# Eight state buffers for heads 1 to 3, stores ahead of the sums, and a distance in the planner for TensorE's work at the ends of six chains

## The chip, the core and the metric

One Trainium2 chip, one of its cores. The metric is the device time of one execution in microseconds (us). TensorE multiplies matrices, VectorE (DVE in the rows) and ScalarE (ACT) do the elementwise work, GpSimd (POOL) does little here, and SyncE (SP) issues nearly all transfers, in one queue, in order.

## The reference

One decoding step of one layer for 512 prompt tokens and 8 sample tokens, which share all weights:

```
z   = rmsnorm(h) @ w_in                     # 1024 -> q,k,v of 12 heads; q,k,v,gates of 4 mLSTM heads
o_a = dilated sliding-window attention      # prompt: 128-wide blocks; samples: rows of three caches
q,k = silu(causal_conv(z_q, z_k))           # mLSTM, 4 heads of 256
samples, each head and sample:
    C_new = w_x * C + w_i * outer(k, v)     # C is 256 x 256, read and written
    num   = q . C_new
prompt: the same recurrence over 512 tokens, as masked products
h  += (sig(ga) * (o_a @ w_pa) + sig(gb) * (o_b @ w_pb)) @ w_out
h  += (silu(x @ w_gate) * (x @ w_up)) @ w_down
h  += sig(x @ w_pg) * (p @ w_pp);  y = rmsnorm(h)
```

All caches and states are outputs too, moved on by one token.

## The kernel before

Activations lie as 128 features by 520 tokens (512 + 8). A weight block of 128 x 128 is split into a high and a low part (`whi`, `wlo`) and meets the two parts of the activations in three matmuls of 260 columns for each half of the tokens; these "dense" matmuls fill most of the time. The list `order` fixes their order: w_in first (attention columns, then the mLSTM heads 0 to 3, then gates), then w_pa, w_pb, w_out, w_gate and w_up, w_down, w_pp, w_pg. The matmuls of w_pb and of most of w_gate and w_up go by Strassen-Winograd products (`wino`), whose raw weights land in buffers of the tags `rp`, `cA`, `cB` (and `WK` later).

All other work is generators ("processes") that the builder steps while it emits the dense matmuls. The class `Clock` estimates, as the program is built, when every engine is done with what was emitted; `on(engines, tiles, tag=n)` gives a condition: n buffers of the tag are free, and the tiles are ready by that estimate. A process goes on when its condition holds; what it emits then stands in the engines' queues at that place, for good. For TensorE (`engs[0] == "pe"`) the condition is that the tiles are ready at the estimated time at which TensorE takes its next matmul:

```
            if engs[0] == "pe":
                t = now
            ...
            return all(ck.ready(x) <= t for x in tiles)
```

If the estimate is early, TensorE comes to the matmul before its operand is there, and waits on the chip; nothing behind it in its queue can pass. If no dense matmul can go on, the builder moves the estimate in steps of 0.1 us (`stall`).

Six ends of chains matter here. `ev_conv` (L950): after the convolution, the tanh and a product with a row of weights (`kw`, in the buffer `yc`, with its sum in `nout`), four transposes of `kw` on TensorE; eight times. `attn_prompt` (L1126): a matmul with `E` and one with `t`, twice each, between small VectorE operations. `attn_sample` (L1201): transposes of the normalised scores `sc`, once (in the trace `scs`). `sample_rows` (L1335): transposes of the sample rows `qkm`, four times. `sample_sums` (L1408): a matmul with `nt`, four times.

The sample states run as a stream beside all this. `sample_loads(h)` (L1353) loads, for each pair of samples, rows of q and k spread over all partitions into the buffers `P1` and `P2` (two each), and for each sample the state `ct` (256 KB) into a buffer of the tag `S` (five). `mlstm_sample(h)` (L1370) scales the state, adds two outer products in place, and then takes two sums over it with q (`tensor_tensor_reduce`, into `numv`); after the sums a process for the store is begun, and the buffer is given back when the store is emitted. The tag `S` also serves the cache rows of `attn_sample` (`kvb`, `qb`) and the rows of `sample_rows`. The loads of heads 1 to 3 begin once `attn_sample` has asked for its last cache rows. After the sums of head 3, `sample_sums` sets `("ns", 3)`, without which no raw weight goes into `cA`; `sample_out` and `pieces` then make the last operand of the first w_pb product.

The tag `rp` (two buffers of 128 x 520) holds the tables `rC` and `rS` of the rotary embedding, read by `ev_rope` (L885) for the last of twelve blocks in the attention columns of half 1; `sw` is a scratch buffer of `ev_rope`. Both tags are free from then until w_pb (`rp`) and the feed-forward layer (`sw`).

Of the kernel before, what the change touches and what calls it, by code (L numbers as in the profile page):

```python
# [8 lines left out]
F32 = mybir.dt.float32  # L9
# [220 lines left out]
def _body(nc, a, const, sb, psp, drp):  # L230
    ck = Clock()
# [4 lines left out]
              P1=2, P2=2, cm=2, on=2, W0=2, W1=2, W2=2, W3=2, hm=2, sm=4, sm48=4,  # L236
              pp=2, b1=4, hf=3)
    WIDTH = dict(cA=640, cB=512, W1=384, W2=256, W3=128, raw=512, hi=512, lo=512, zc=ZC, yc=ZC - 3)
    used = dict.fromkeys(("pp", "G", "WK", "b1", "z", "y", "zc", "yc", "S", "P1", "P2", "cm", "hm", "hf", "sw"), 0)

    def tl(tag, name, shape=None, dt=F32):
        w = WIDTH.get(tag, 520)
        if tag in used:
            used[tag] += 1
        return ck.new(sb.tile(list(shape or (128, w)), dt, name=name, tag=tag, bufs=NB[tag]), tag, NB[tag])

# [17 lines left out]
    def free(n, tag):  # L264
        used[tag] -= n
# [2 lines left out]

    P = dict(PAR["A"])

    def on(engs, *tiles, lim=None, **rooms):

        engs = engs.split()

        def ok():
            for tag, n in rooms.items():
                if tag in used and used[tag] + n > NB[tag]:
                    return False
            now = ck.t["pe"]
            for tag, n in rooms.items():  # L280
                i = ck.count.get(tag, 0)
                if any(ck.idle(tag, i + j, NB[tag]) > now + P["SLACK"] for j in range(n)):
                    return False
            if engs[0] == "pe":
                t = now
            else:
                t = min(ck.t[e] for e in engs)
                if t > now + (P["LIM"] if lim is None else lim):
                    return False
                t = max(t, now) + 0.1  # L290
            return all(ck.ready(x) <= t for x in tiles)
        return ok
# [271 lines left out]
    def dma_chunk():  # L564
        c = dma_at[0]
        j, ci = order[c]
        dma_at[0] += 1
        if "src" in j:
            for b in j["load"].get(ci, ()):
                tag = next(j["tags"])  # L570
                wlast[tag, ck.count.get(tag, 0) % NB[tag]] = c - ci + WLAST[b]
                j["raw"][b] = tl(tag, "raw", (128, 4, 128))[:, :j["nk"]]
                SP.dma_start(j["raw"][b], j["src"][b])
            return
        src, _, n = j["chunks"][ci]
        if j["keep"] and (j["keep"], ci) in kept:
            return
        if j["keep"]:
            kept[j["keep"], ci] = None
        raw = tl("raw", "raw", (128, 4, 128))  # L580
        SP.dma_start(raw[:, :n, :j["M"]], src)
        raws[c] = raw
# [182 lines left out]
    eps_t = const.tile([128, 1], F32, name="eps_t")  # L765
    ident = cstA[:, C_ID:C_ID + 128]
    rC, rS = tl("rp", "rC"), tl("rp", "rS")
    rb = const.tile([128, 520], F32, name="rb")
    flag = {}
    HS = [slice(h * TH, h * TH + TH) for h in range(2)]  # L770
# [114 lines left out]
    def ev_rope(kind, g, i):  # L885
        def gen(ps):
            yield on("dve", rC, rS, ps, lim=P["EVLIM"], z=1, sw=1)
            z = tl("z", "z")
            sw = tl("sw", "sw")
            V.stream_shuffle(p2(sw), ps, SW)  # L890
            V.tensor_tensor(p2(z), ps, p2(rC), op=ALU.mult)
            free(1, "pp")
            yield on("dve", sw)
            mul(sw, sw, rS)
            yield on("dve", sw, z)
            add(z, z, sw)
            free(1, "sw")
            if g == 0:
                yield on("act dve", z, G=2)
                hi, lo = (tl("G", "qk"[kind] + x, (128, TP), F32R) for x in "hl")  # L900
                split(hi, lo, z[:, :TP])
                attn[kind, g, i] = hi, lo
            else:
                yield on("act dve", z, G=1)
                t = tl("G", "qk"[kind] + "r", (128, TP))
                copy(t.rearrange("p (r j) -> p r j", r=4), z[:, :TP].rearrange("p (j r) -> p r j", r=4))
                attn[kind, g, i] = t,
            G_.tensor_copy((qs, ks)[kind][:, i, g], z[:, TP:])
            if kind == 1:
                yield on("sp", z)  # L910
                SP.dma_start(a["kT"][2 * g + i], z)
            free(1, "z")
        return gen
# [36 lines left out]
    def ev_conv(h, w, dt):  # L950
        m = 8 * w + 2 * h + dt

        def gen(ps):
# [28 lines left out]
            if w == 0:  # L982
                free(1, "yc")
            else:
                kw = y[:, :TP]
                yield lambda: h in wkbs
                yield on("dve", y, wkbs[h])
                V.tensor_tensor_reduce(kw, kw, wkbs[h], sc, 0.0, ALU.mult, ALU.add, nout[:, h, dt, 0:1])
                if dt == 1:
                    free(1, "y")  # L990
                yield on("pe", kw, b1=1, WK=2)
                hi = tl("WK", "kwh", (128, 4, 128), F32R)
                lo = tl("WK", "kwl", (128, 4, 128), F32R)
                bk = bank((128, 4, 128))
                for s in range(4):
                    PE.transpose(bk[:, s], kw[:, s * 128:(s + 1) * 128], ident)
                free(1, "yc")
                yield on("act dve", bk)
                split(hi, lo, bk)
                free(1, "b1")  # L1000
                ml["kw", h, dt] = hi, lo
# [119 lines left out]
    done = {}  # L1121
# [4 lines left out]
    def attn_prompt(i):  # L1126
# [12 lines left out]
        yield on("dve", *st, y=1)  # L1139
        E = tl("y", "E", (128, 512))  # L1140
        V.tensor_copy(E.rearrange("p (j r) -> p j r", r=4), ident.unsqueeze(2).to_broadcast([128, 128, 4]))
        yield on("pe", E, b1=1)
        al = bank((128, 4, 2, 2, 4))
        for qb in range(4):
            PE.matmul(al[:, qb].rearrange("p c h r -> p (c h r)"),
# [24 lines left out]
        for lay in range(2):  # L1170
# [2 lines left out]
        t = one(32, "t32").rearrange("p (q h r) -> p q h r", q=4, h=2)  # L1173
        V.tensor_tensor(t, ex[:, 1].unsqueeze(3).to_broadcast([128, 4, 2, 4]),
                        cstB[:, C_R4:C_R4 + 4].unsqueeze(1).unsqueeze(1).to_broadcast([128, 4, 2, 4]), op=ALU.mult)
        yield on("pe", t, b1=1)
        w1 = bank((128, 2, 4))
        for qb in range(4):
            PE.matmul(w1.rearrange("p h r -> p (h r)"), cstB[:, C_Z + 96 - 32 * qb:C_Z + 224 - 32 * qb],
# [21 lines left out]
    def attn_sample():  # L1201
# [59 lines left out]
        for g in range(3):  # L1261
            yield on("pe", le)
            for i in range(2):
# [18 lines left out]
        rsv = rs[0:32].rearrange("p (g b) -> p g b", g=3)  # L1282
        V.tensor_tensor(rsv, cstB[0:32, C_M8:C_M8 + 8].unsqueeze(1).to_broadcast([32, 3, 8]),
                        sc[:, :, 128:129].to_broadcast([32, 3, 8]), op=ALU.mult)
        yield on("pe", sc, b1=1)
        bk = bank((128, 3, 32))
        for g in range(3):
            PE.transpose(bk[:, g], sc[:, g, 0:128], ident[0:32, 0:32])
# [42 lines left out]
    junk = const.tile([128, 256], mybir.dt.bfloat16, name="junk")  # L1331

    mdr, cts, qks = {}, {}, {}

    def sample_rows(h):  # L1335

        yield lambda: all(("k", h, dt) in ml for dt in range(2)) and "rows" in flag
        yield on("pe", qkm, b1=1, S=1)
        bk = bank((8, 2, 2, 128))
        rows = tl("S", "mrows", (8, 2, 256))  # L1340
        for w in range(2):
            for dt in range(2):
                PE.transpose(bk[:, w, dt], qkm[:, h, w, dt], ident)
        yield on("act dve", bk)
        copy(rows.rearrange("b w d -> b (w d)"), bk.rearrange("b w t d -> b (w t d)"))
        free(1, "b1")
        yield on("sp", rows)
        dr = drp.tile([8, 2, 256], F32, name="mdr", tag="mdr", bufs=2)
        SP.dma_start(dr.rearrange("b w d -> b (w d)"), rows.rearrange("b w d -> b (w d)"))
        free(1, "S")  # L1350
        mdr[h] = dr

    def sample_loads(h):  # L1353

        yield lambda: h in mdr
        dr = mdr[h]
        for b in range(8):
            if b % 2 == 0:
                yield on("sp", dr, P1=1, P2=1)
                qb, kb = tl("P1", "qb", (128, 2, 256)), tl("P2", "kb", (128, 2, 256))  # L1360
                SP.dma_start(qb, dr[b:b + 2, 0].partition_broadcast(128))
                SP.dma_start(kb, dr[b:b + 2, 1].partition_broadcast(128))
                qks[h, b] = qb, kb
            yield on("sp", S=1)
            ct = tl("S", "ct", (128, 2, 256))
            SP.dma_start(ct, a["sC"][h, b])
            cts[h, b] = ct
        flag["loads", h] = True

    def mlstm_sample(h):  # L1370
# [7 lines left out]
        def steps(b0):  # L1378
            for b in range(b0, 8, 2):
# [8 lines left out]
                for vt in range(2):  # L1388
                    yield on("dve", cur, kb, vw)
                    stt(cur[:, vt], kb[:, b % 2], vw[:, vt, b:b + 1], cur[:, vt], ALU.mult, ALU.add)  # L1390
                for vt in range(2):
                    yield on("dve", cur, qb)
                    V.tensor_tensor_reduce(junk, cur[:, vt], qb[:, b % 2], 1.0, 0.0, ALU.mult, ALU.add,
                                           numv[:, vt, b:b + 1])
                left[0] -= 1
                done[b] = True
                if b ^ 1 in done:
                    free(1, "P1")
                    free(1, "P2")
                store(a["C_s"][h, b], cur, lambda: free(1, "S"))  # L1400

        done = {}
        for b0 in range(2):
# [4 lines left out]
    def sample_sums(h, numv):  # L1408
# [8 lines left out]
        V.tensor_tensor(nn, nn, tv, op=ALU.add)  # L1417
        V.tensor_tensor(tv, nn, qkm[:, h, 0], op=ALU.mult)
        V.tensor_tensor(nt[:, :, 8:16], numv, numv, op=ALU.mult)
        yield on("pe", nt, b1=1)  # L1420
        bk = bank((128, 16))
        for t in range(2):
            PE.matmul(bk, ones, nt[:, t], start=t == 0, stop=t == 1)
# [388 lines left out]
    def pair_src(name, q):  # L1812
        return {f"{r + 1}{k + 1}": a[name][2 * q + r, k] for r in range(2) for k in range(2)}

    wok["cA"] = lambda: "scores" in flag and "oas" in flag and ("ns", 3) in ml and 1 in oaf
    wok["WK"] = lambda: order_pos[0] >= n_pa

# [463 lines left out]
```

## Time and profile before

| | |
|---|---|
| time, median of 3 runs | 1072.8 us (1072.44 to 1077.44) |
| profiled execution: its time, its span | 1072.9 us, 1071.1 us |
| TensorE matmul busy, share of the span | 1041.0 us, 97% |
| VectorE busy, ScalarE busy | 848.3 us (79%), 518.3 us (48%) |
| mean granted TensorE clock | 0.99 |
| HBM read, written | 163.65 MB, 59.13 MB |

The span is from the first to the last instruction; the time of the execution is 1.8 us longer. Busy time is the sum over an engine's instructions; matmuls overlap and their ends are modelled, so a busy TensorE need not run at its peak. The granted clock is 1.00 at 2.4 GHz and 0.50 at 1.2 GHz.

### The profile page before, as it was taken

The numbers are of one execution on the slowest core, as the hardware profiler recorded it, in microseconds if no ns is written. First come the engines' busy times: TensorE is split into PE (matmuls) and PEld (weight loads), VectorE is DVE, ScalarE is ACT, GpSimd is POOL, SyncE is SP. The second block draws the span as 40 slices with busy tenths as digits, with TensorE's granted clock in tenths as the row PEclk, the third lists the DMA queues.
The fourth block names the chain that finished last, engine by engine and source line by source line (L and its number), as shares of the span: only waits on it lengthen the run. The fifth ranks groups of instructions, "written<-read, shape, count | busy, mean of one in ns | idle before, by whom it ended". The sixth has DMA issues, their size and how long they took to land.

```text
span 1071.1 us, 21842 instructions
## 1 busy us (share of the span) xinstructions
PE 1041.0 (97%) x8440; PEld 1022.7 (95%) x8440; DVE 848.3 (79%) x1749; ACT 518.3 (48%) x963; POOL 40.8 (4%) x126
## 2 busy tenths in 40 slices
PE   8999999999998999999999999999999999999996
PEld 7999999898997999999999999999999999999995
DVE  6994678877797698998457588989788888866685
ACT  6534644555454477776333345444334334433652
POOL 0010010001010021000000000000000000000000
PEclk9999999999997999999999999999999999999999
DMA  6456247774865876987666743422332332333331
GB/s 227 129 181 211 85 147 261 258 223 155 265 192 179 294 268 230 296 273 259 219 204 230 257 125 87 145 79 75 114 113 76 114 111 75 108 91 105 99 110 60
DMA packets 91191, 180.21 MB, mean 168 GB/s; under 512 B 11636, under 2 KB 37796, under 8 KB 89680
## 3 DMA queue, kind: packets, MB, share of 16 engines
q1 hardware_dynamic: 90512, 178.29, 51.6%
q8 instruction: 66, 1.08, 0.4%
q10 hardware_dynamic: 576, 0.53, 0.1%
q14 instruction: 37, 0.30, 0.1%
HBM read 163.65 MB, written 59.13 MB: 208 GB/s over the span
## 4 chain that ended last, share of the span: by engine, by line
PE 77%; DVE 12%; DMA 5%; ACT 3%; issue 2%; SPq 0%; POOL 0%; DVEq 0%; ACTq 0%
PE pp L225 45%; PE b L225 32%; DMA raw<-in_w_in 2%; DVE wlo L225 2%; DMA ct<-in_sC 2%; DVE yc L225 2%; DVE ct L225 1%; DVE sw L225 1%; DVE Wf L225 1%; ACT whi L225 1%; DVE z L225 1%; DVE junk L225 1%; SPq L225 0%; DMA kvb<-in_cache 0%; DMA xr<-in_xT 0%
## 5 line engine op out<-in xcount | busy, mean ns | idle before, releaser
L225 ACT CAST whi<-raw 128x512 fp32r<-128x512 f32 (+3 forms) x344 | 204.9, 599 | 279.9 <-PE pp L225 146.3
L225 DVE TENSOR_TENSOR wlo<-raw,whi 128x512 fp32r<-128x512 f32 (+3 forms) x359 | 236.3, 661 | 129.4 <-ACT whi L225 121.2
L225 PE MATMUL b<-piece,whi 128*128 128x260 f32 x1176 | 212.3, 282 | 1.5 <-DVE whi L225 1.4
L225 PE MATMUL pp<-xnh,whi 128*128 128x260 f32 x992 | 204.2, 287 | 0.0
L225 PE MATMUL pp<-xnh,wlo 128*128 128x260 f32 x992 | 203.5, 287 | 0.0
L225 PE MATMUL pp<-xnl,whi 128*128 128x260 f32 x992 | 199.7, 283 | 0.0
L225 PEld LDWEIGHTS b<-piece,whi 128*128 128x128 f32 x1176 | 181.3, 188 | 1.9 <-issue 1.9
L225 PE MATMUL b<-piece,wlo 128*128 128x260 f32 x588 | 166.3, 283 | 0.1
L225 PEld LDWEIGHTS pp<-xnh,wlo 128*128 128x128 f32 x992 | 153.7, 190 | 1.0
L225 PEld LDWEIGHTS pp<-xnh,whi 128*128 128x128 f32 x992 | 153.0, 189 | 1.3
L225 PEld LDWEIGHTS pp<-xnl,whi 128*128 128x128 f32 x992 | 153.5, 189 | 0.0
L225 PEld LDWEIGHTS b<-piece,wlo 128*128 128x128 f32 x588 | 110.7, 188 | 0.4 <-DVE wlo L225 0.4
L225 PE MATMUL pp<-hpl,whi 128*128 128x260 f32 x352 | 71.1, 283 | 0.0
L225 PE MATMUL pp<-hph,whi 128*128 128x260 f32 x352 | 70.9, 283 | 0.0
L225 PE MATMUL pp<-hph,wlo 128*128 128x260 f32 x352 | 70.7, 282 | 0.0
L225 PEld LDWEIGHTS pp<-hph,wlo 128*128 128x128 f32 x352 | 54.4, 188 | 0.0
L225 PEld LDWEIGHTS pp<-hpl,whi 128*128 128x128 f32 x352 | 54.3, 188 | 0.0
L225 PEld LDWEIGHTS pp<-hph,whi 128*128 128x128 f32 x352 | 54.2, 188 | 0.0
L225 ACT CAST whi<-ws 128x512 fp32r<-128x512 f32 x28 | 17.4, 622 | 57.0 <-PE b L225 48.8
L225 DVE TENSOR_TENSOR uv<-uv,b 128x260 f32<-128x260 f32 (+1 forms) x84 | 40.8, 486 | 0.0
L225 DVE SCALAR_TENSOR_TENSOR yc<-zc,par,yc 128x552 f32<-128x552 f32 x48 | 37.8, 788 | 3.4 <-ACT yc L225 2.9
L225 PE MATMUL b<-x3h,wlo 128*128 128x260 f32 x128 | 36.7, 287 | 0.0
(387 smaller groups left out, 1933.3 us busy)
## 6 DMA issues: line engine op xcount, KB each, us to landing
raw<-in_w_in SPq DMA_DIRECT2D x132, 256.0 KB, 2.8
out_kvout<-in_cache SPq DMA_DIRECT2D x64, 512.0 KB, 4.8
raw<-in_w_gate SPq DMA_DIRECT2D x44, 256.0 KB, 2.9
raw<-in_w_up SPq DMA_DIRECT2D x44, 256.0 KB, 4.2
ct<-in_sC SPq DMA_DIRECT2D x32, 256.0 KB, 6.7
out_C_s<-ct SPq DMA_DIRECT2D x32, 256.0 KB, 4.9
raw<-in_w_down SPq DMA_DIRECT2D x32, 256.0 KB, 2.7
out_kvout<-in_cache SPq DMA_DIRECT2D x16, 510.0 KB, 3.9
```

The source lines that it names most:

```text
L225: fn(*args, **kw)
```

## The change

1. `on` gets `lead`: for TensorE the tiles must be ready, by the planner's estimate, at `now - lead`. It is 1.0 us at the transposes of `kw`, 0.8 us at the other five ends.
2. Of the eight states of each of the heads 1 to 3, the first two go to `rp`, the third to `sw`, five to `S`. Head 0 keeps `S`. `rp` is now counted: given back after the twelfth rotary block, taken for states, and raw weights of w_pb go to it only when the loads of head 3 are all emitted and no state holds it (`wok["rp"]`). Raw weights are not counted (`count=False`).
3. The process that stores a state is begun after the two outer products, ahead of the two sums. The buffer is given back when both the store and the sums are emitted (`both`, `release`).

```
-    def on(engs, *tiles, lim=None, **rooms):
+    def on(engs, *tiles, lim=None, lead=0.0, **rooms):
...
-                t = now
+                t = now - lead
...
+            ropes.append(z)
+            if len(ropes) == 12:
+                free(2, "rp")
...
-                yield on("pe", kw, b1=1, WK=2)
+                yield on("pe", kw, lead=1.0, b1=1, WK=2)
...
-        yield on("pe", E, b1=1)
+        yield on("pe", E, lead=0.8, b1=1)
...
-        yield on("pe", t, b1=1)
+        yield on("pe", t, lead=0.8, b1=1)
...
-        yield on("pe", sc, b1=1)
+        yield on("pe", sc, lead=0.8, b1=1)
...
+    release = {}
+
+    def both(cur, n):
+
+        left, tag = [n], ck.slot[cur.tensor.name][0]
+
+        def done():
+            left[0] -= 1
+            if not left[0]:
+                free(1, tag)
+        release[cur.tensor.name] = done
+        return done
...
-        yield on("pe", qkm, b1=1, S=1)
+        yield on("pe", qkm, lead=0.8, b1=1, S=1)
...
-            yield on("sp", S=1)
-            ct = tl("S", "ct", (128, 2, 256))
+            tag = ("rp", "rp", "sw", "S", "S", "S", "S", "S")[b] if h else "S"
+            yield on("sp", **{tag: 1})
+            ct = tl(tag, "ct", (128, 2, 256))
...
+                store(a["C_s"][h, b], cur, both(cur, 2))
...
-                store(a["C_s"][h, b], cur, lambda: free(1, "S"))
+                release[cur.tensor.name]()
...
-        yield on("pe", nt, b1=1)
+        yield on("pe", nt, lead=0.8, b1=1)
...
+    wok["rp"] = lambda: ("loads", 3) in flag and used["rp"] == 0
```

## Rows read from the trace of the kernel before

**Rows 1.** The page, part 1: busy us (share of the span) and instructions

```profile
PE 1041.0 (97%) x8440; PEld 1022.7 (95%) x8440; DVE 848.3 (79%) x1749; ACT 518.3 (48%) x963; POOL 40.8 (4%) x126
```

**Rows 2.** What TensorE waited for: total us, times, longest us

```profile
PE b L225 <- DVE nout L225: 6.6, 4, 3.8
PE b L225 <- DVE t L225: 1.6, 2, 1.3
...
PE b L225 <- DVE W2l L225: 1.0, 2, 0.6
...
PE b L225 <- DVE scs L225: 0.8, 1, 0.8
...
PE b L225 <- DVE E L225: 0.2, 1, 0.2
PE b L225 <- POOL qkm L225: 0.2, 1, 0.2
```

**Rows 3.** Stages of 50 us: length, busy per engine, clock, DMA share, GB/s

```profile
300.00:350.00 50.00, 44.59 (x321) 42.98 (x320) 41.86 (x95) 23.65 (x40) 5.56 (x17) 0.84 0.57 180
...
400.00:450.00 50.00, 48.70 (x392) 47.51 (x390) 44.92 (x113) 36.20 (x66) 3.26 (x9) 1.00 0.84 266
...
500.00:550.00 50.00, 50.00 (x420) 50.00 (x419) 34.08 (x59) 18.94 (x34) 0.00 (x0) 1.00 0.63 211
```

**Rows 4.** Stages of 5 us around the two falls of the clock

```profile
315.00:320.00 5.00, 5.00 (x28) 4.72 (x27) 4.39 (x9) 2.02 (x4) 1.48 (x3) 0.66 0.23 64
...
335.00:340.00 5.00, 1.93 (x16) 1.71 (x15) 2.77 (x6) 1.95 (x2) 0.47 (x1) 0.70 0.82 236
340.00:345.00 5.00, 4.24 (x21) 4.28 (x21) 4.89 (x10) 1.96 (x3) 0.00 (x0) 0.50 0.65 209
345.00:350.00 5.00, 5.00 (x25) 4.68 (x25) 4.85 (x15) 1.72 (x3) 0.00 (x0) 0.50 0.46 161
350.00:355.00 5.00, 5.00 (x41) 5.00 (x41) 4.76 (x17) 1.32 (x4) 0.37 (x1) 0.93 0.47 154
```

**Rows 5.** Timeline of TensorE: start, us, matmul [idle before, releaser]

```profile
255.21 1.03 PE L225 MATMUL b<-t,cstB 128*128 128x8 f32 x8 [1.31 <-DVE t L225]
...
274.98 0.66 PE L225 MATMUL b<-cstA,yc 128*128 128x128 f32 x4 [0.34 <-DVE nout L225]
...
285.35 0.66 PE L225 MATMUL b<-cstA,yc 128*128 128x128 f32 x4 [1.31 <-DVE nout L225]
285.76 0.48 PE L225 MATMUL pp<-xnh,wlo 128*128 128x260 f32 x2
...
340.76 1.09 PE L225 MATMUL b<-cstA,yc 128*128 128x128 f32 x4 [3.83 <-DVE nout L225]
341.63 5.12 PE L225 MATMUL b<-pT,kvb 128*128 128x2 f32 x24
...
407.82 0.63 PE L225 MATMUL b<-cstA,yc 128*128 128x128 f32 x4 [1.17 <-DVE nout L225]
```

**Rows 6.** Timeline of VectorE ahead of the wait at 285.35

```profile
283.26 0.69 DVE L225 TENSOR_TENSOR wlo<-raw,whi 128x512 fp32r<-128x512 f32 x1
```

**Rows 7.** Timeline of SyncE's queue: the stream of states, w_pb's weights

```profile
422.28 0.29 SPq L225 DMA_DIRECT2D mdr<-mrows  x1
...
434.66 0.46 SPq L225 DMA_DIRECT2D qb<-mdr  x1
...
465.91 0.58 SPq L225 DMA_DIRECT2D ct<-in_sC  x1
...
484.29 2.15 SPq L225 DMA_DIRECT2D raw<-in_w_pb  x4
```

**Rows 8.** Timeline: head 3's last state sum, its last operand, TensorE's use

```profile
481.18 0.42 DVE L225 CUSTOM_DVE_ANT_0 junk<-ct,qb 128x256 bf16<-128x256 f32 x1
...
494.01 0.42 DVE L225 TENSOR_TENSOR piece<-th,piece 128x260 fp32r<-128x260 f32 x1
...
498.46 0.40 PE L225 MATMUL b<-piece,whi 128*128 128x260 f32 x2
```

More of the change, by code (lines that the diff above doesn't have):

```diff
@@ L238, in _body, with tl @@
     WIDTH = dict(cA=640, cB=512, W1=384, W2=256, W3=128, raw=512, hi=512, lo=512, zc=ZC, yc=ZC - 3)
-    used = dict.fromkeys(("pp", "G", "WK", "b1", "z", "y", "zc", "yc", "S", "P1", "P2", "cm", "hm", "hf", "sw"), 0)
-    def tl(tag, name, shape=None, dt=F32):
+    used = dict.fromkeys(("pp", "G", "WK", "b1", "z", "y", "zc", "yc", "S", "P1", "P2", "cm", "hm", "hf", "sw", "rp"), 0)
+    def tl(tag, name, shape=None, dt=F32, count=True):
         w = WIDTH.get(tag, 520)
-        if tag in used:
+        if tag in used and count:
             used[tag] += 1
@@ L571, in dma_chunk @@
                 wlast[tag, ck.count.get(tag, 0) % NB[tag]] = c - ci + WLAST[b]
-                j["raw"][b] = tl(tag, "raw", (128, 4, 128))[:, :j["nk"]]
+                j["raw"][b] = tl(tag, "raw", (128, 4, 128), count=False)[:, :j["nk"]]
                 SP.dma_start(j["raw"][b], j["src"][b])
@@ L767, in _body @@
     rC, rS = tl("rp", "rC"), tl("rp", "rS")
+    ropes = []
     rb = const.tile([128, 520], F32, name="rb")
```

## The prediction

> **What bounds the kernel now.** I first read the page's busy times [rows 1]: TensorE is busy for 1041.0 of 1071.1 us, so whatever the change does to other engines, it can give back at most the 30 us that TensorE idles and what it loses while its clock is low. Then the view of what TensorE waited for [rows 2]. It has 20 rows, from `nout` to `qkm`, which add up to 21 us (the rest of the 30 is the tail after the last matmul). The reader is to see which releasers are at the ends that get a lead: `nout` (the transposes of `kw`) 6.6, `t` 1.6, `scs` 0.8, `E` 0.2, `qkm` 0.2, in all 9.4 us in 9 waits; `nt` has no row, so nothing was waited for there. Third the stages of 50 us [rows 3]: from 300 to 350 TensorE is busy for 44.6 us and the clock's mean is 0.84, while at 500 to 550 it is 50.0 and 1.00. So what can be won lies before some 450 us, and most of it around 340. The stages of 5 us there [rows 4] show 28 matmuls at 315 to 320, and 16, 21 and 25 at 335 to 350, with clock 0.50 to 0.70; 41 matmuls fit at 350 to 355 with a clock of 0.93.
>
> What the low clock costs can be worked out from these rows. (1 - clock) x 5 us is 1.7 at 315 to 320, and 1.5 + 2.5 + 2.5 + 0.35 = 6.85 at 335 to 355. In the second stretch TensorE also idles for 3.83 us [rows 5], and an idle engine loses nothing by its clock: half of 3.83, 1.9, comes off. The clock therefore costs 1.7 + 4.9 = 6.6 us there.
>
> **The leads.** A lead adds no instruction. The same matmuls go into TensorE's queue later, behind about 1.0 or 0.8 us (in the planner's time) of other matmuls. Whether this removes a wait depends on whether other matmuls could run. At 285.35 they could: the dense matmul behind the transposes at 285.76 [rows 5] takes a `wlo`, and VectorE's last `wlo` before the wait began at 283.26 and took 0.69, so it ended at 283.95 [rows 6], 1.4 us before the transposes. The waits of 0.34 and 1.17 at 274.98 and 407.82 look the same, with dense work on both sides. I take from each wait its own length, at most its lead: `nout` 0.34 + 1.0 + 1.0 + 1.0 = 3.34 of its four waits of 0.34, 1.31, 3.83 and 1.17; `t` 0.8 of 1.31 and the whole other 0.3, 1.1; `scs` 0.8; `E` and `qkm` 0.2 each. The sum is 5.6 us, and 3.8 of the 9.4 stay, 2.8 of them at 340.76. Bounds: 0, if the re-dealt order puts the waits elsewhere, and 9.4, if the operands are in time by chance too. I take 5.6, since in three of the four `nout` waits and the longer `t` wait dense matmuls follow at once.
>
> What is late next: the products of `kw`, the buffer `yc` and the sums behind `t` and `scs` all come about 1 us later. The only queue in which these matmuls stand is TensorE's; ScalarE and VectorE have the evacuation of the transposed `kw` behind them, and go on with other work by the planner's order. `yc` held 1 us longer would make the evacuation of the next convolution's sums late; in the 20 rows of waits none is for an evacuation of such sums, so there is room for 1 us. If that room were gone the cost is 1 us at each of eight transposes, 8 us.
>
> **The clock.** The fall at 335 to 355 goes with the wait of 3.83 us, and also with 24 matmuls of 2 columns that stand in a row right behind it, 5.12 us long [rows 5]. The fall at 315 to 320 has only short work and the one `scs` wait of 0.8 near it. With a lead there is more dense work in both places, but the thin ones stay. So between nothing and all of the 6.6 us comes back; no row tells which, both falls being mixed, and I take the middle, 3.3.
>
> **The states.** Bytes and instructions are the same: 24 loads and 24 stores of 256 KB for heads 1 to 3, two outer products and two sums each. What changes is when. The rows of head 3 went out at 422.28, but its first load of q and k stands at 434.66 [rows 7], behind states of head 2 that still held `P1` and `P2`; these have two buffers each as before, so no more than two pairs of samples are in flight, and eight buffers only take the stores out of the way. I put the stream 0 to 12 us earlier. Does TensorE gain by it? Head 3's last sum ends at 481.6, the last operand for w_pb is written at 494.01 + 0.42 = 494.4, and TensorE takes it at 498.46 or later [rows 8]: it is in time by 4 us, and no wait stands there. So an earlier stream is worth nothing by itself, only more room; a stream later by x us would cost x - 4. The stores now ask SyncE to wait for the outer products in place of the sums; behind them in that queue stand weight loads, but the wait begins and ends earlier by the two sums, so nothing is added. The new condition on `rp`: w_pb's weights went out at 484.29 [rows 7], 2.7 us after the last sum, because `cA` was held for head 3 already. The two `rp` states are the first of their head and are done sooner, so the condition ends before the old one. All this counts 0, covered by the 4 us at 498.
>
> **The sum.** 1072.9 (the profiled execution, 1071.1 of span and 1.8 around it, 0.1 above the median) - 5.6 - 3.3 = 1064.0 us.
>
> **Rivals.**
>
> *The waits move.* The order of all that the builder emits follows from its estimates, so the first displaced matmul re-deals all that is emitted after it, as long as chains run beside the dense matmuls. Ends that get no lead cost now: `W2l` 1.0 [rows 2], and with `W3l`, `z`, `o_sb`, the two parts of `sqh`, `kvb` and the pieces of w_pb about 6 of the 21 us. If a new deal doubles these, and a fall of the clock like the first (1.7) stays, the gain is 8.9 - 6 - 1.7 = 1 us: 1071.7. For it: VectorE is late against the estimate by up to 3.8 us, more than any lead. Against it: nothing in the change makes these ends worse on the whole.
>
> *The clock comes back whole at 340.* If the fall at 335 to 355 is the work of the 3.83 us wait alone [rows 4, 5], shortening it gives 4.9 us there and nothing at 315: 5.6 + 4.9 = 10.5 us, 1062.4. Against it: at 315 to 320 the clock fell to 0.66 with TensorE busy for 5.00 of 5 us [rows 4], so idle time is not the only cause. The Trainium skill (TensorE: Matmul & The Clock Gate, section "HAM oscillation — how this bites in real kernels") ties the lower clock to long idle gaps, which is this rival; the row at 315 to 320 does not agree with it.
>
> *Slower: VectorE crowded by the stream.* From 400 to 450 VectorE is busy for 44.9 of 50 us [rows 3], and the convolutions of head 3 run there. A stream that starts more states at a time puts outer products and sums in front of a convolution's chain, and TensorE waits for `kw` as it does at 340.76: 3.8 + 4.9 of clock = 8.7 us each. One such place where there is none now eats the gain (1072.7), two make 1081.4. It decides as soon as VectorE is more than about 4 us late at two convolutions. For it: the busy share. Against it: between 355 and 450, where most of the states are done now, the only `nout` wait is that of 1.17.
>
> *The change does little:* the leads count by the estimate, and if the estimate is late by more than a lead wherever it is late, only the short waits go: 0.34 + 0.3 + 0.2 + 0.2 + 0.8 = 1.8 us, 1071.1. The four long waits, of which three are no more than 0.5 above their lead, speak against it.
>
> **Chances.** The forecast, a gain of 5.5 to 16 us (1057 to 1067.4): 0.55, of which 0.12 is the rival with the whole clock, whose time lies inside. Moved waits or little done, 1067.5 to 1078: 0.31. Slower: 0.14. A measurement of this kernel tells about 0.5%, 5.4 us, from no change, so faster means below 1067.4 and slower above 1078.2. The best case is 9.4 + 6.6 = 16 us, 1057. The range is to leave out 2 in 10: its lower end is 1056, with 1 us of luck at other ends; its upper end is 1075, which leaves out the slower cases and the worst of the unchanged.
>
> **What the profile after would show.** Right: the wait view's `nout` row at or below 3.5 us and `t`, `scs`, `E` and `qkm` together below 1; the clock of 300 to 350 above 0.84; TensorE's busy time lower by the 3.3 us of clock; the last state store before 484, and no wait at the first w_pb product. Wrong: a new `nout` wait of more than 2 us after 350, rows of `W2l`, `z` or `whi` that together exceed 10 us, or a clock below 1.00 in a stage that has 1.00 now.

## The result, and the profile after

The changed kernel takes 1078.33 us (median of 19 runs, 1074.57 to 1085.92), the kernel before, beside it, 1072.8 (19 runs): a ratio of 1.0051 [1.0036, 1.0066]. The prediction was 1064.0 with a range of 1056 to 1075. So the change made the kernel slower by 5.5 us where a gain of 9 was forecast.

The page's busy line of the kernel after, the line that answers to [rows 1]:

```profile
PE 1045.4 (97%) x8440; PEld 1026.3 (95%) x8440; DVE 847.9 (79%) x1753; ACT 516.8 (48%) x959; POOL 41.4 (4%) x126
```

The span is 1076.5 us, 5.4 more than before. TensorE is busy for 4.4 us more with the same 8440 matmuls. In the trace it works for 20.5 us at the lower clock, where it was 13.3 us before; at half the speed that costs half of the difference, 3.6 of the 4.4 us. What it waited for (total us, times, longest):

```profile
PE b L225 <- ACT z L225: 4.6, 5, 2.5
PE b L225 <- DVE t L225: 3.4, 1, 3.4
PE b L225 <- DMA kvb<-in_cache: 2.7, 4, 1.2
...
PE b L225 <- DVE nt L225: 1.1, 1, 1.1
...
PE b L225 <- ACT sqhh L225: 1.1, 1, 1.1
```

Against [rows 2], the rows of `nout`, `scs`, `E` and `qkm` are gone: of 9.4 us at the ends with a lead, 3.4 (`t`) and 1.1 (`nt`) are left, a saving of 4.9 where 5.6 was forecast. But the whole view again adds up to 21.8 us, against 21: the rows at ends without a lead rose from 11.6 to 17.3 us. `z`, the cache rows `kvb` and `sqhh` have taken the place.

The stages of 50 us, and of 5 us around the falls of the clock (columns as in [rows 3, 4]):

```profile
250.00:300.00 50.00, 46.39 (x373) 45.18 (x372) 42.93 (x92) 23.47 (x48) 7.43 (x23) 0.97 0.71 222
300.00:350.00 50.00, 47.27 (x331) 45.62 (x330) 33.90 (x74) 24.95 (x41) 5.06 (x20) 0.86 0.49 161
350.00:400.00 50.00, 46.30 (x368) 45.06 (x367) 39.58 (x111) 28.82 (x55) 5.31 (x18) 1.00 0.79 263
...
550.00:600.00 50.00, 48.37 (x387) 47.76 (x386) 32.63 (x58) 18.01 (x33) 0.00 (x0) 0.97 0.65 226
...
310.00:315.00 5.00, 2.80 (x19) 2.53 (x19) 0.69 (x1) 1.68 (x3) 0.00 (x0) 1.00 0.96 299
315.00:320.00 5.00, 5.00 (x25) 4.71 (x26) 0.00 (x0) 0.88 (x2) 0.00 (x0) 0.66 0.17 59
...
340.00:345.00 5.00, 5.00 (x25) 5.00 (x25) 2.79 (x8) 3.84 (x7) 0.72 (x3) 0.50 1.08 426
```

The two stages that now have a clock of 0.97 had 1.00 before:

```profile
250.00:300.00 50.00, 46.30 (x378) 44.74 (x377) 38.96 (x75) 23.11 (x43) 6.75 (x25) 1.00 0.75 241
...
550.00:600.00 50.00, 48.07 (x394) 47.22 (x394) 34.41 (x61) 18.15 (x33) 0.00 (x0) 1.00 0.65 225
```

The wait of 3.83 us at 340.76 is gone, and TensorE is busy for 5.00 of 5 us at 340 to 345, and yet the clock is at its lower level there. Now it lowers the speed of work, where before it fell partly on an idle engine. Nor had that wait brought the clock down: in the trace of before the last matmul ahead of it ends at 336.9, the clock is 1.00 up to 337.0, and at 337.0 to 337.5, with the wait just begun, it is 0.52.

How the largest new wait of `z` arises, in a timeline (start, us, engine, operation, idle before and what ended it):

```profile
362.35 0.72 ACT L225 ACTIVATE ct<-ct,s24b 128x512 f32<-128x512 f32 x1 [2.49 <-DMA ct<-in_sC]
362.98 0.60 ACT L225 CAST whi<-raw 128x512 fp32r<-128x512 f32 x1
...
363.49 0.58 ACT L225 COPY z<-pp 128x520 f32<-128x520 f32 x1
...
364.12 0.66 PE L225 MATMUL b<-cstA,z 128*128 128x128 f32 x4 [2.48 <-ACT z L225]
```

A state's scaling stands in ScalarE's queue ahead of its load, and ScalarE waits 2.49 us for the transfer. The evacuation that writes `z` is queued behind it, and TensorE waits 2.48 us for `z`. In all, ScalarE waits for state loads like this:

```profile
ACT ct L225 <- DMA ct<-in_sC: 15.6, 9, 3.9
```

In the kernel before, the same row of the same view says 11.9 us in 9 waits. The `t` wait is another matter. VectorE's part of that chain, and TensorE behind it:

```profile
258.72 0.22 DVE L225 TENSOR_TENSOR t<-b,cstB 128x64 f32<-128x64 f32 x1
...
261.88 0.19 DVE L225 TENSOR_TENSOR t<-ex,cstB 128x32 f32<-128x32 f32 x1
...
262.21 1.03 PE L225 MATMUL b<-t,cstB 128*128 128x8 f32 x8 [3.41 <-DVE t L225]
```

The chain begins at 258.72 and takes 3.4 us, with two operations of other chains among its own. No other matmul is queued between the chain's begin and its end, so a lead of 0.8 does not reach; in the new order TensorE stands still for all of it.

**Clock or waits?** Every run lists its mean granted clock, so times can be compared at one clock. A line through the 81 runs of the kernel before that stand beside the experiments gives 1836.6 - 773.4 x clock (us), from which those runs scatter by 1.4. The 19 runs after lie 5.4 +- 0.9 us above this line, at a mean clock of 0.9865 against 0.9855. I call this distance the excess: what is lost at an equal mean clock. So over all runs it is not a lower mean clock that separates the two kernels.

The two profiled executions (mean clock 0.987 and 0.990) can be taken apart. Of the 5.4 us between their spans, 1.1 is idle time of TensorE (21.6 us against 20.6 between its first and last matmul). Another 3.6 is the lower clock on a busy TensorE (above): before, 3.7 us of the lower clock fell on idle time and cost nothing, after, none, which makes 1.9 of the 3.6; the other 1.7 is that there is more of it (20.5 us in all against 17.1). The averages over all runs do not show this last part, so it may belong to these two executions alone. The 0.8 left stands in no row. (All are sums over the records of the matmuls and of the clock, up to the last matmul.) At an equal clock the pair differs by 5.4 - 0.003 x 773 = 3.1 us, and not by the 5.4 of the average, because the profiled execution of before itself lies 2.2 us above the line.

### The profile page after: what moved, and what is told of

It is laid out like the page before. It is cut to its first block, busy times and chain, and to the rows that moved or that the text cites. A ratio compares the mean times of both kernels' runs of the same rounds, so it can differ in the third digit from the quotient of the medians.

```text
span 1076.5 us, 21795 instructions
## 1 busy us (share of the span) xinstructions
PE 1045.4 (97%) x8440; PEld 1026.3 (95%) x8440; DVE 847.9 (79%) x1753; ACT 516.8 (48%) x959; POOL 41.4 (4%) x126
## 4 chain that ended last, share of the span: by engine, by line
PE 63%; DVE 10%; DMA 5%; ACT 3%; issue 3%; SPq 1%; POOL 0%; DVEq 0%; ACTq 0%
PE pp L225 35%; PE b L225 28%; DMA ct<-in_sC 4%; DVE wlo L225 2%; DVE ct L225 1%; SPq L225 1%; DVE yc L225 1%; DVE junk L225 1%; DMA raw<-in_w_in 1%; DMA kvb<-in_cache 1%; DVE Wf L225 1%; ACT whi L225 1%; ACT ct L225 0%; ACT zc L225 0%; DVE th L225 0%
## 5 line engine op out<-in xcount | busy, mean ns | idle before, releaser
L225 ACT CAST whi<-raw 128x512 fp32r<-128x512 f32 (+3 forms) x339 | 201.9, 598 | 283.7 <-PE pp L225 153.9
```

The lines of the kernel that those rows point to most:

```text
L225: fn(*args, **kw)
```

## The experiments

Each table row is a kernel of the sections below: ratio to the kernel before on the same chip, median, excess (above), mean clock of its runs, and when SyncE issued the very last state load in the profiled execution, in a group of two its second (before: 465.9, after: 467.5). The excess has an interval of +-0.4 to 1.8.

| kernel | ratio [95%] | us | excess | clock | last load |
|---|---|---|---|---|---|
| leads_only | 1.0035 [1.0012, 1.0057] | 1078.6 | 1.5 | 0.982 | 463.7 |
| states_only | 1.0031 [1.0003, 1.0059] | 1078.8 | 2.1 | 0.983 | 469.3 |
| no_early_store | 1.0043 [1.0021, 1.0065] | 1079.8 | 2.7 | 0.982 | 468.4 |
| five_buffers | 1.0076 [1.0049, 1.0103] | 1082.6 | 10.6 | 0.987 | 477.8 |
| leads_fifth | 1.0141 [1.0110, 1.0172] | 1090.2 | 13.1 | 0.981 | 490.1 |
| thin2_before | 1.0138 [1.0104, 1.0171] | 1090.8 | 15.3 | 0.985 | 487.2 |
| thin2_after | 1.0164 [1.0131, 1.0197] | 1092.9 | 17.6 | 0.984 | 482.5 |
| late_loads | 0.9992 [0.9966, 1.0018] | 1073.4 | 3.0 | 0.989 | 457.5 |
| late_before | 1.0067 [1.0044, 1.0090] | 1080.4 | 5.7 | 0.984 | 470.7 |
| late_leads_only | 1.0187 [1.0160, 1.0214] | 1094.5 | 11.9 | 0.976 | 494.4 |
| late_states_only | 1.0216 [1.0189, 1.0242] | 1097.4 | 17.8 | 0.979 | 489.9 |
| late_both | 1.0074 [1.0052, 1.0096] | 1081.6 | 7.5 | 0.986 | 476.8 |
| local_leads | 0.9986 [0.9968, 1.0005] | 1072.4 | -1.2 | 0.986 | 464.7 |
| lead_at_340 | 1.0092 [1.0062, 1.0122] | 1084.3 | 10.2 | 0.986 | 463.2 |
| t_lead_4 | 1.0083 [1.0051, 1.0114] | 1082.9 | 11.2 | 0.989 | 470.3 |
| no_head1 | 1.0002 [0.9980, 1.0025] | 1074.7 | -4.6 | 0.980 | 456.3 |

Where an expectation names a theory by a letter: B is that any other deal of the order is worse than that of before; D that groups of thin matmuls bring the clock down; E that the planner takes loads of states to be early, which costs by itself; F that a late end of the stream of states makes TensorE wait at 485 to 500.

**The parts of the change.** leads_only is the kernel before with the leads alone; states_only has `t = now` for `t = now - lead`; the other two are the kernel after, with these edits:

```
# no_early_store: the store begins after the sums again
-                store(a["C_s"][h, b], cur, both(cur, 2))
...
-                release[cur.tensor.name]()
+                store(a["C_s"][h, b], cur, both(cur, 1))
# five_buffers
-            tag = ("rp", "rp", "sw", "S", "S", "S", "S", "S")[b] if h else "S"
+            tag = "S"
```

> Before, with the six leads alone. If the states cost the gain (theory A): the waits at the six ends fall from 9.4 us to below 4.5 and nothing takes their place, 1064 to 1068 us, some 5 to 8 below before. If any new deal of the order puts other waits in their place (theory B): the same fall at the six ends, but other waits and low clock make up for it, 1070 to 1080. If late operands are made later by the leads (theory C): as the full change, 1076 to 1080, with t and z waits as there.

> The full change with every lead at 0. Theory A: slower than before by 5 or more, 1078 to 1084, with new waits of TensorE on ScalarE's z behind a scaling of a state that waits for its load. Theory B: anywhere from 1069 to 1081, its nout waits still there. Theory C: as before, 1070 to 1075.

> The full change, but the store of a state is begun after its two sums, as before. If the early store is what hurts (SyncE waits on it ahead of weights and loads): 1070 to 1074. If the eight buffers are: as the full change, 1077 to 1080. Theory B: another deal, within 1069 to 1081, and its waits are not those of the full change.

> The full change, but all states of all heads go to the five S buffers (early stores and leads stay). If the eight buffers hurt: 1066 to 1072, near the leads alone. If the early store does: 1077 to 1080. Theory B: another deal, within 1069 to 1081, and its waits are not those of the full change.

No part is good by itself: leads and states alone each cost 0.3%. In leads_only only 2.0 us are left at the ends with a lead, less than forecast, and others have grown; three rows of its waits:

```profile
PE b L225 <- ACT z L225: 4.1, 4, 2.7
PE b L225 <- DVE W3l L225: 1.9, 1, 1.9
PE b L225 <- DMA kvb<-in_cache: 1.5, 1, 1.5
```

With an excess of 1.5 and a clock lower by 0.0033 (2.5 us on the line above), most of what it loses is clock. states_only loses 1.7 of its 3.8 by clock; its stage of 300 to 350:

```profile
300.00:350.00 50.00, 45.86 (x298) 43.25 (x296) 37.00 (x82) 22.03 (x38) 5.90 (x17) 0.78 0.55 173
```

The early store is worth nothing that can be told (1.0043 without it, 1.0051 with it). The eight buffers do what they are for: with five, the last load goes out 10 us later and the excess is 10.6, not 5.4 (the medians differ by 4.3 us). The first four waits of five_buffers:

```profile
PE b L225 <- ACT z L225: 4.6, 5, 2.3
PE b L225 <- DVE t L225: 3.4, 1, 3.4
PE b L225 <- DVE nt L225: 2.4, 1, 2.4
PE pp L225 <- ACT th L225: 2.3, 2, 1.6
```

`z` and `t` are those of the kernel after; `nt` and `th` are larger or new, and belong to the stream of states: `nt` is an end of its sums, and `th` is the evacuation of the gates that w_pb's operands are made from.

**The size of a lead, and the thin matmuls.** leads_fifth is leads_only with leads of 0.2 and 0.16 us. The thin matmuls are the products of the cached v, in groups (three in the program, six in the trace); the planner lets 0.8 us of other TensorE work between two groups, and thin2_before and thin2_after (made from the kernels before and after) ask for 2.0:

```
-    "A": dict(LIM=1.8, SLACK=1.5, THIN=0.8,
+    "A": dict(LIM=1.8, SLACK=1.5, THIN=2.0,
```

> Before, with leads of 0.2 at the transposes of kw and 0.16 at the other five ends: a fifth, too short to cover more than 0.2 us of any wait. If before owes its time to a lucky deal of the order (theory B): slower than before like the four others, 1075 to 1081, by waits and low clock at places of its own. If the size of the leads or the state edits carry the loss: within 0.2% of before, 1071 to 1075.

> Before, with THIN in the first set of parameters 2.0 in place of 0.8: the planner puts 2.0 us between the groups of three matmuls of 2 columns of attn_sample, so that dense matmuls stand between them. If rows of these matmuls bring the low clock at 315 to 350 (theory D): low clock there falls from 17 us to below 7, and the mean clock over the runs rises above 0.988; time 1066 to 1071. If waits alone bring it: low clock as before, 0.984 to 0.988, time 1071 to 1081 by the new deal.

> The full change with THIN 2.0. Theory D: low clock at 313 to 350 falls from 13.7 us to below 7, 1070 to 1075. If waits alone bring the low clock: 1076 to 1082.

A lead of 0.2 us costs more than one of 1.0: how large the lead is does not order the results. (The largest of its waits is `th`, 9.8 us.) Three of the thin groups in thin2_after, its stage of 300 to 350, and its first wait:

```profile
316.06 0.78 PE L225 MATMUL b<-pT,kvb 128*128 128x2 f32 x6
318.21 0.72 PE L225 MATMUL b<-pT,kvb 128*128 128x2 f32 x6
320.32 0.72 PE L225 MATMUL b<-pT,kvb 128*128 128x2 f32 x6
```

```profile
300.00:350.00 50.00, 49.04 (x402) 48.16 (x400) 38.96 (x75) 24.91 (x43) 6.34 (x23) 1.00 0.53 163
```

```profile
PE pp L225 <- ACT th L225: 10.5, 3, 8.1
```

With a group every 2.1 us and dense matmuls between them, the clock of this stage stays at 1.00 where it was 0.84 before and 0.86 after, and TensorE is busy for 49 of 50 us; thin2_before has 0.97 there. But the samples' products then end later, the stream of states with them, and TensorE waits 8.1 us for `th` at 487.6. The time was lost again 150 us further on, and so was the clock: over the runs its mean is 0.985 and 0.984, no higher than before, where theory D wanted above 0.988. Theory D fits the stage that it is about. It is not shown that the close groups are what brings the clock down, since late_loads (next) keeps them and has nearly the same clock there:

```profile
300.00:350.00 50.00, 45.99 (x361) 44.66 (x360) 38.49 (x85) 25.92 (x43) 5.88 (x19) 0.97 0.60 199
```

Between 316 and 336 its trace has eleven groups in three clusters, in each of which they begin 0.9 to 1.3 us apart, and the clock is 1.00 throughout. Each of these clocks is of one execution.

**Holding the scalings back.** Four kernels tell the planner that a load of a state lands 4 us later, so ScalarE gets the scaling later: late_loads (from the kernel after), late_before, late_leads_only and late_states_only. late_both is late_loads, with the cache rows 3 us later too.

```
             SP.dma_start(ct, a["sC"][h, b])
+            for k in ck.keys(ct):
+                ck.wr[k]["dma"] += 4.0
```

> The full change, with the planner's estimate of the landing of each sample state 4.0 us later, so that the scaling of a state is put into ScalarE's or VectorE's queue when the load has landed more often. If scalings that wait for their load hold up evacuations that TensorE needs (z at 354.8 and 364.1, 3.7 us): ScalarE's waits for state loads fall below a half, the z waits below 1.5 us, and the time to 1072 to 1076. If these waits are only a matter of the deal: other waits of the same sum, 1076 to 1082.

> Before, with the estimated landing of each sample state 4.0 us later. If early estimates of these loads are a cost of their own (theory E): ScalarE's waits for state loads go to about 0 as in the run with the full change, and the time is 1066 to 1072 with before at 1073 to 1077. If it is a new deal and nothing else (theory B): 1073 to 1085.

> The six leads alone, with the later estimate. Theory E: below the leads alone (1.0035 of before), 0.993 to 1.000. Theory B: 1.000 to 1.010. In either the waits at the six ends stay below 5 us. If the end of the stream of states decides (theory F): over before by what its last state load comes after some 467 us.

> The eight buffers and early stores without the leads, with the later estimate. Theory E: below the same without it (1.0031 of before), 0.994 to 1.001. Theory B: 1.000 to 1.010. Theory F: by its last state load; with eight buffers that is before 467, so not above before.

> The full change with the later estimate for states, and 3.0 us later for the cache rows (keys and values) of attn_sample, for which VectorE waits ahead of the t wait at 262 (3.4 us) and TensorE at 313 to 315 (2.2 us). Theory E: these two waits fall below 2 us together, 1066 to 1072, ratio below 0.997. Against it: attn_sample then asks for its last rows later, the stream of states begins and ends later, and by theory F the time goes up by what its last load comes after 467 us.

In late_loads ScalarE's waits for states fall from 15.6 us to 0.8, and the time is that of before, with an excess of 3.0 at a higher mean clock. But the waits for `z`, which should have fallen below 1.5, are still 3.2 of 4.6. The same edit on the kernel before takes those waits of ScalarE from 11.9 to 0.2, and makes it 0.7% slower; on the two halves of the change it leaves 3.8 and 4.0, and costs 1.5 and 1.9% more. late_both keeps the `t` wait of 3.4. So those waits are not what decides, and theory E falls. What the two halves share is a stream that ends late (494.4 and 489.9, where theory F expected before 467 for late_states_only), and waits for `th`, 17.1 and 5.1 us. late_before has neither: its last load is at 470.7, and its largest waits are `t` 4.1 and `nout` 3.5.

**The end of the stream.** no_head1 is late_leads_only without the states of head 1: their 8 loads, scalings, products, sums and stores are left out, which takes that work off VectorE and ScalarE too.

```
-        for b in range(8):
+        for b in range(0 if h == 1 else 8):
...
-            for b in range(b0, 8, 2):
+            for b in range(b0, 0 if h == 1 else 8, 2):
```

> The leads alone with the later estimate (ratio 1.0187, TensorE waits 15.5 us at 498 for the evacuation of a gate), with the states of head 1 left out: 8 loads, their scalings, products, sums and stores. If the end of the stream is the cause (theory F): the last state load comes 20 us or more earlier than 494, the 15.5 us wait is gone, ratio 1.000 to 1.008. If the cause is the deal around the gates: a wait of 7 us or more stays at 480 to 500, ratio above 1.012.

The timelines of late_leads_only, with SyncE's last load, VectorE's last sums before the wait, ScalarE's `th` and TensorE:

```profile
491.76 2.99 SPq L225 DMA_DIRECT2D ct<-in_sC  x2
...
496.73 0.42 DVE L225 CUSTOM_DVE_ANT_0 junk<-ct,qb 128x256 bf16<-128x256 f32 x1
497.19 0.60 ACT L225 ACTIVATE th<-pp 128x520 f32<-128x520 f32 x1 [1.40 <-DVE numv L225]
...
497.85 0.80 PE L225 MATMUL pp<-xnh,whi 128*128 128x260 f32 x2 [15.50 <-ACT th L225]
```

and the first two waits of no_head1:

```profile
PE pp L225 <- DVE wlo L225: 3.3, 3, 1.9
PE b L225 <- ACT P L225: 1.5, 1, 1.5
```

TensorE's accumulators for the gates (`pp`) come free when they are evacuated into `th`. `th` lies in a buffer of `P1` or `P2`, which the rows of q and k of the last states hold until their sums are done: the sum of 496.73 ends at 497.15, `th` starts at 497.19, TensorE at 497.85. With a shorter stream (last load at 456.3) there is no wait for `th` at all, and the excess falls from 11.9 to -4.6, by 16.5, about the 17.1 us that the row of `th` showed in late_leads_only (15.5 and 1.6); in the profiled executions TensorE idles 16 us less (15.6 against 31.5). The table agrees over all kernels: whatever issues its last load after 476 has an excess of 7.5 us or more. (The reverse does not hold: lead_at_340 and t_lead_4, below, have 10.2 and 11.2 with last loads at 463.2 and 470.3.)

**Leads in single places.** local_leads is the kernel before with a lead of 1.3 at the transposes of `kw` of head 1 and of head 3's first half alone; lead_at_340 has one of 4.0 at head 2's second half alone (the wait of 3.83). t_lead_4 is the kernel after with 4.2 at the second `t`.

```
# local_leads
-                yield on("pe", kw, b1=1, WK=2)
+                yield on("pe", kw, lead=1.3 * (h == 1 or h == 3 and dt == 0), b1=1, WK=2)
# lead_at_340
+                yield on("pe", kw, lead=4.0 * (h == 2 and dt == 1), b1=1, WK=2)
# t_lead_4
-        yield on("pe", t, lead=0.8, b1=1)
+        yield on("pe", t, lead=(0.8, 4.2)[i], b1=1)
```

> Before, with a lead of 1.3 at three transposes of kw alone (both of head 1, the first of head 3), where before waits 0.34, 1.31 and 1.17 us. TensorE's queue differs from before in 160 lines of some 4,700 rows only, and is the same again after each. If leads do what they say where the order behind them stays (theory G): these three waits go, no other appears, 1.5 to 3 us faster, ratio 0.997 to 0.9990. If a lead only moves the wait to the next operand: ratio 1.000 to 1.002.

> Before, with a lead of 4.0 at the second transposes of kw of head 2 alone, where before waits 3.83 us and the clock falls. The order is the same up to there and dealt anew behind it. Theory G: the wait of 3.83 and its low clock go (3.8 + 4.9 us), but the new deal gives some back: ratio 0.992 to 1.002. If the end of the stream (theory F) gets later than 467 us by it, above 1.003.

> The full change with a lead of 4.2 in place of 0.8 at the t matmul of the second half, where it waits 3.4 us at 262. Theory G: that wait goes; the order behind is a new deal, so 1.000 to 1.010 of before, with other waits at other places; if that wait were the whole of the loss, 1.001 or below.

In local_leads the order is nearly the old one: of TensorE's 8440 matmuls in the trace, 98 stand at another place than before (by tile and shape, in order of start), where it is 1,377 in leads_only and 1,531 in the kernel after. Its first three waits:

```profile
PE b L225 <- DVE nout L225: 4.3, 1, 4.3
PE b L225 <- ACT z L225: 1.7, 4, 0.7
PE b L225 <- DVE t L225: 1.6, 2, 1.3
```

The three waits of 0.34, 1.31 and 1.17 are gone, 2.8 us; 0.5 comes back at 339.8 (4.3 for 3.83), and 0.8 and 0.6 at `z` and `qkm`. The excess is -1.2 +- 0.4 and the wait for `whi` that stands at 586.6 before stands at 585.5. It is the fastest kernel here, though the ratio's interval still holds 1. lead_at_340 takes the 3.83 us away and gets this in return:

```profile
357.70 0.72 ACT L225 ACTIVATE ct<-ct,s24b 128x512 f32<-128x512 f32 x1 [7.42 <-DMA ct<-in_sC]
...
361.09 0.59 ACT L225 COPY z<-pp 128x520 f32<-128x520 f32 x1
...
361.74 0.47 PE L225 MATMUL b<-cstA,z 128*128 128x128 f32 x1 [5.01 <-ACT z L225]
```

ScalarE stands 7.42 us at a state's load, and `z` is late by 5.01. In t_lead_4 the 3.4 us of `t` are gone too, and its first three waits are

```profile
PE b L225 <- ACT vmh L225: 2.6, 1, 2.6
PE pp L225 <- ACT th L225: 2.1, 2, 1.1
PE b L225 <- ACT piece L225: 2.1, 1, 2.1
```

6.8 us in places where the kernel after waits for nothing. The excess is 11.2, and most of it these rows do not explain: all of its waits add up to 23.4 us, 2.4 more than before.

## Why the prediction was wrong

**The leads (5.6 forecast): right at their ends, wrong as a gain.** 4.9 us of the 9.4 went, and where the order is nearly held (local_leads) closed waits turn into time in part, 1.2 us of 2.8 at an equal clock. The step that failed is the one behind the sum, that beside these ends nothing changes: the waits at ends without a lead rose by 5.7 us (11.6 to 17.3). The rival "the waits move" named this mechanism (the first displaced matmul re-deals all that follows) and sized it nearly right, at 6. It still came to a gain of 1 us, 1071.7, because it too counted clock as won, 3.3 - 1.7 = 1.6 us.

The deal of before is a good one among those tried: of the 16 others in which no work is left out, local_leads, which nearly keeps it, and late_loads come out level, and the other fourteen lose 0.3 to 2.2%, the changed kernel 0.5. Even single leads that close the wait they are aimed at (lead_at_340, t_lead_4) lose 0.9 and 0.8% against before, and t_lead_4 0.3% against the kernel after, from which it is made.

**The clock (3.3 forecast): nothing came back.** This is the second step that failed. The clock of 300 to 350 rose from 0.84 to 0.86, but two stages that had 1.00 now have 0.97, which the prediction had named as a sign of being wrong, and TensorE's busy time grew by 4.4 us: in the profiled pair the lower clock cost 3.6 us more in place of 3.3 less. I took the middle between two causes, the wait and the thin matmuls. It was not the wait. Before, the clock fell as the wait began (337.0); lead_at_340 takes the wait away and its clock over the runs is 0.986 as before. The thin matmuls, which the change left in their groups, are the likelier cause, and not shown: spacing them went with 1.00 at 300 to 350 (thin2_after), but late_loads has 0.97 with close groups. What brings the falls stays open, so this term had no row to stand on and should have been 0. The rival in which the clock comes back whole at 340 fails on the same rows: at 340 to 345 the clock is 0.50 with TensorE busy for 5.00 us. The Trainium skill (TensorE: Matmul & The Clock Gate, section "HAM oscillation — how this bites in real kernels") lays the lower clock to long idle gaps; this trace does not agree at 339.2, where the clock fell after 0.5 us of idle time in 10 us, in gaps of 0.23 and 0.27. It fits the fall at 264.1, which follows the `t` wait of 3.41 us.

Together, in the profiled pair, idle time of 1.1 more in place of 5.6 less and the clock's 3.6 more in place of 3.3 less are 13.6 of the 14.3 us between forecast and measurement.

**The states (0 forecast): the room was right, the direction wrong.** The stream was put 0 to 12 us earlier; its last load went out at 467.5, 1.6 later than before, the last sum ended 1.5 later, and no wait stands at w_pb's first product, as forecast. The later stream is paid for elsewhere: TensorE waits 1.1 us for `nt`, behind the last sums, at 484.45, an end at which before waited for nothing. That a stream which is much too late is paid for is shown by late_leads_only against no_head1 (which also has less work for VectorE and ScalarE), though what waits there is `th`, for a buffer that the stream holds, and not the operand `piece`. Against five buffers in the same kernel the eight are worth 5 us of excess, since the re-dealt order runs later. They insure against a stream that the order of before does not have.

**The rival on the slower side** named VectorE, with new waits for `nout`. There are none. Of the new waits that were followed up, that for `z` goes through ScalarE's queue, where a scaling stands ahead of its load.

**What stays open.** What brings the clock down at 300 to 350, and whether the kernel after has more of the lower clock than its one trace shows, stays open; so does the rest of the excess of 5.4 us beyond the 3.1 of the profiled pair. The `z` and the `t` wait of the kernel after were never undone with the rest of its order held: each edit that removed one dealt anew. And why this order of before is good was not settled, only that all but two of the edits tried lose it.

## What to carry to other kernels

Where a planner deals the order of all engines' work, a local fix is priced by what it re-deals, and not by the wait it closes: look first at how much of the emitted order it leaves in place, and time a few small edits, whose spread is the yardstick (here fourteen of sixteen lost 0.3 to 2.2%). Before a term for the clock is counted, look at what came first, the wait or the fall (here the clock fell as the wait began), and count nothing where no row tells what brings the fall. A load's consumer in an in-order queue delays all that stands behind it, so look for evacuations behind it.

## What had not been expected of the hardware

The clock fell with TensorE at work nearly all the time: to 0.50 at 339.2 in the kernel after, where 340 to 345 has 25 matmuls in 5.00 of 5 us. In late_loads it fell at 307.0, with no idle time of TensorE in the trace since 293.8. The same thin matmuls of 2 columns, in groups of six every 2.1 us with dense ones between, left it at 1.00 for 50 us (thin2_after, 402 matmuls against 331); but so did closer groups in late_loads from 316 to 336.
